# The output projection of layer 2: plain for 256 tokens, a block scheme of seven products for the rest

## The chip, the cores and the metric

The kernel runs on one core of one Trainium2 chip. Its engines work side by side and meet through semaphores: TensorE (PE, with its weight loads as PEld), VectorE (DVE), ScalarE (ACT), GpSimd (POOL) and SyncE (SP), whose queue issues most DMAs. Each engine does its instructions in the order in which they stand in its program. The metric is device time in microseconds of one launch; lower is better.

## The reference

One inference step of two layers for 1024 prompt tokens and 8 decode rows, all in float32. Layer 1 is a retention layer, layer 2 sliding-window attention with 16 heads of 64. What matters here is the end of layer 2:

```
def swa_layer(x, ...):
    ...
    o = swa_attend_prompt(q, k, v, sinks)       # (tokens, 1024)
    ...
    o = o * jax.nn.silu(gate)
    return x + o @ w_out, new_k, new_v          # w_out: 1024 x 1024
```

The projection has 1024 outputs, 1024 inputs and 1032 columns (1024 prompt tokens and 8 decode rows).

## The kernel before

Float32 products are made of three matmuls each: every operand is split into a high part (rounded) and a low part (the rest), and hi x hi, hi x lo and lo x hi are added up in PSUM (`proj`, L1710). ACT makes high parts, DVE or POOL the low parts. Data stand transposed, features on the partitions and tokens along the columns. `A_hi` and `A_lo` (SA in the profile) hold the eight k-tiles of 128 features of the moving operand.

Layer 2's attention is a loop written out by hand over 35 steps (L2504). In a step, scores of one block of 128 tokens are made (`att_s`), softmax runs on DVE, ACT and POOL (`att_e`, `att_p`, `att_r`), and for a block two steps back the values are multiplied (`att_o`) and gated (`att_out`, L2133) and split into hi and lo (`att_split`, L2143). Heads go in two groups: the outputs of group 0 (k-tiles 0 to 3) wait in DRAM as hi and lo (`oscr_h`, `oscr_l`) and are loaded back by `reload3` (L2253), since their place in `A_hi` still holds the layer's input; those of group 1 (k-tiles 4 to 7) are written to `A_hi` and `A_lo` directly. The decode rows' attention runs between the last steps (`STEPS`, L2495): `dec_scores`, `dec_soft`, `dec_pt`, `dec_o`, `dec_out` (L2247), which writes 8 columns of `A_hi`/`A_lo`.

Between the small matmuls of a step, `fill` gives PE pieces of larger work: first the input projections of layer 2, then the output projection, `so_all` (L2309). It has 24 tasks: 8 feature tiles of 128 x 3 token groups of 384, 384 and 264 columns, each 8 k-tiles x 3 matmuls. A task's accumulator is one PSUM bank (`pj`); `finish` (L2346) adds the residual (`xr`, L2359) and DVE transposes and SP or ACT stores the result (`so_y`, L2275) with four DMAs of 32 partitions. Six tasks run inside attention, eighteen behind it. Weights come in slots of 256 features (`wslot`, L1655): four loads of 256 KB, a high part by ACT (L1674), a low part by POOL (L1675), paced by `job` (L1683); three slots fit.

What is in no planner is set by the order in which this code calls the engines; the four engines besides PE also keep that order.

Of the kernel before, what the change touches and what calls it, by code (L numbers as in the profile page):

```python
# [15 lines left out]
NP = 1024  # L16
# [56 lines left out]
def _trunk(ctx, tc, nc, a):  # L73
# [23 lines left out]
    oscr_l = dp.tile([4, 128, NP], F32, name="oscr_l")  # L97
    pbs = dp.tile([8, 128, 640], F32, name="pbs")
# [1688 lines left out]
    atp = ctx.enter_context(tc.tile_pool(name="atp", bufs=1))  # L1787
# [345 lines left out]
    def att_out(u):  # L2133
        po, gt = u.po, G[u.g, u.ti]
        ot = atq[0].tile([128, 512], F32, name="ot", bufs=1)
        nc.vector.scalar_tensor_tensor(ot.rearrange("p (a y) -> p a y", a=4), po[:, :, 0:128], 0.5,
                                       gt[:, 512 * u.i:512 * u.i + 512].rearrange("p (a y) -> p a y", a=4),
                                       ALU.mult, ALU.mult)
# [108 lines left out]
    def dec_out():  # L2247
        nc.vector.scalar_tensor_tensor(god, god, 0.5, gdec2, ALU.mult, ALU.mult)
        nc.vector.tensor_copy(A_hi[:, :, NP:NT], god)
        nc.vector.tensor_tensor(A_lo[:, :, NP:NT], god, A_hif[:, :, NP:NT], ALU.subtract)  # L2250
        oready[2] = True

    def reload3(ti):  # L2253

        t0, t1 = TG[ti]
        t1 = min(t1, NP)
        for o_, src in ((A_hif, oscr_h), (A_lo.bitcast(F32), oscr_l)):
            nc.sync.dma_start(out=o_[:, 0:4, t0:t1], in_=src[:, :, t0:t1].rearrange("k p t -> p k t"))
# [6 lines left out]
    nso = [0]  # L2265
    attn = [True]
# [5 lines left out]
    pend_y, yds = [], []  # L2272
    LAST = ((7, 1), (7, 2))

    def so_y(ft, ti, yt):  # L2275
        t0, t1 = TG[ti]
        npr = min(t1, NP) - t0
        nch = npr // 128
        if (ft, ti) not in LAST:
            yo = atp.tile([128, 384], F32, tag="qs", name="yo", bufs=6)  # L2280
            nc.vector.transpose(yo[:, :npr], yt[:, :npr])
            st = nc.sync if attn[0] else nc.scalar
            for q in range(4):
                f0 = ft * 128 + 32 * q
                st.dma_start(
                    out=y_p[0, t0:t0 + npr, f0:f0 + 32].rearrange("(b r) c -> r b c", r=32),
                    in_=yo[32 * q:32 * q + 32, :npr].rearrange("r (b c) -> r b c", c=32))
            if ti == 2:
                nc.vector.transpose(yds[0][:, ft, :], yt[:, 256:288])
                if ft == 6:  # L2290
                    for q in range(4):
                        nc.scalar.dma_start(
                            out=y_s[:, 0, 0:896].rearrange("t (f c) -> t f c", c=128)[:, :, 32 * q:32 * q + 32],
                            in_=yds[0][32 * q:32 * q + 8])
            return
        pt = trp.tile([128, 512], F32, name="tr")
        for i in range(nch):
            tr(pt[:, i * 128:i * 128 + 128], yt[:, i * 128:i * 128 + 128], ident)
        if ti == 2:
            tr(pt[:8, 256:384], yt[:, 256:264], ident)  # L2300
# [320 lines left out]
```

## Time and profile before

| | us |
|---|---|
| median of 3 runs (1221.51 to 1223.53) | 1221.83 |
| the profiled execution | 1222.17 |
| its span, first to last instruction | 1220.3 |
| PE busy in the span | 1209.4 |
| 850 to 950: input projections of layer 2 begin, PE / DVE / ACT / POOL busy of 100 | 100.0 / 46.3 / 50.3 / 58.5 |
| 950 to 1146: attention, PE / DVE / ACT / POOL busy of 196 | 195.9 / 132.3 / 95.5 / 100.7 |
| 1146 to 1215: rest of the output projection, PE / DVE / ACT / POOL busy of 69 | 69.0 / 19.6 / 2.7 / 5.7 |

Times in rows are microseconds from the span's start. A group of instructions is told as line, engine, operation, what it writes and reads, count, then busy time and mean ns of one, then the engine's idle time just before them and what ended it. A busy PE is not PE at its peak: matmuls overlap, so starts are compared, not lengths. A wait for several things is put down to the one that came last.

### The profile page before, as it was taken

Reading aid. Unit: us, or ns where it says so; the run is one execution under the profiler, and the core shown is the slowest. Engines: PE = TensorE matmul, PEld = TensorE weight load, DVE = VectorE, ACT = ScalarE, POOL = GpSimd, SP = SyncE. Lnnn points to the kernel's source line nnn. Section 1 sums busy time; section 2 is a strip of 40 time slices with the busy share of each in tenths; the row PEclk is TensorE's granted clock in tenths of the full one; section 3 lists DMA queues with packets and bytes.
Section 4 is the critical chain, followed back from the end, with each engine's and each line's share of the span. In section 5 each row is a group of like instructions: output and inputs, shape, how many; then the busy total and the mean of one; then the engine's idle time right before and its main releaser. Section 6 shows DMA issues by size and latency. Waiting matters only on the chain.

```text
span 1220.3 us, 29346 instructions
## 1 busy us (share of the span) xinstructions
PE 1209.4 (99%) x11261; PEld 1148.0 (94%) x11261; DVE 733.2 (60%) x1425; ACT 590.2 (48%) x1518; POOL 693.1 (57%) x761
## 2 busy tenths in 40 slices
PE   8999999999999999999999999999999999999998
PEld 6999999999999999998888999999999999999998
DVE  6954656556656667357777455767435666677422
ACT  6533445535545556367877123446444545545100
POOL 5654544445527999968977145782656627654010
PEclk9999999999999999999999999999999999999999
DMA  6313866767676686365687894685531346246554
GB/s 227 110 52 118 247 190 214 223 205 220 205 237 185 194 242 188 109 199 185 216 251 215 246 261 151 195 250 155 137 117 65 115 133 174 90 140 181 135 125 86
DMA packets 260219, 213.18 MB, mean 175 GB/s; under 512 B 72953, under 2 KB 231093, under 8 KB 260062
## 3 DMA queue, kind: packets, MB, share of 16 engines
q1 hardware_dynamic: 215040, 180.72, 50.3%
q10 hardware_dynamic: 45038, 30.57, 8.3%
q8 instruction: 89, 1.46, 0.5%
q14 instruction: 52, 0.43, 0.1%
HBM read 139.10 MB, written 73.17 MB: 174 GB/s over the span
## 4 chain that ended last, share of the span: by engine, by line
PE 91%; DVE 3%; POOL 2%; DMA 1%; issue 1%; ACT 1%; ACTq 0%; SPq 0%; POOLq 0%; DVEq 0%
PE S L1346 10%; PE pj L1717 8%; PE b L340 8%; PE b L342 7%; PE b L341 7%; PE pj L1719 7%; PE pj L1718 7%; PE b L333 4%; PE b L334 4%; PE b L335 4%; PE xy L2070 2%; PE tr L109 2%; PE o L2128 2%; PE b L556 1%; PE S L341 1%; PE S L340 1%
## 5 line engine op out<-in xcount | busy, mean ns | idle before, releaser
L340 PE MATMUL b<-xh,woh 128*128 128x258 f32 x784 | 223.6, 285 | 0.0
L342 PE MATMUL b<-xh,wol 128*128 128x258 f32 x784 | 221.5, 283 | 0.1
L341 PE MATMUL b<-xl,woh 128*128 128x258 f32 x784 | 221.4, 282 | 0.0
L1717 PE MATMUL pj<-SA,wh 128*128 128x384 f32 (+1 forms) x576 | 189.6, 329 | 0.1
L1719 PE MATMUL pj<-SA,wl 128*128 128x384 f32 (+1 forms) x576 | 184.8, 321 | 0.0
L1718 PE MATMUL pj<-SA,wh 128*128 128x384 f32 (+1 forms) x576 | 184.2, 320 | 0.0
L340 PEld LDWEIGHTS b<-xh,woh 128*128 128x128 f32 x784 | 147.8, 188 | 4.1 <-issue 4.1
L341 PEld LDWEIGHTS b<-xl,woh 128*128 128x128 f32 x784 | 148.8, 190 | 0.0
L342 PEld LDWEIGHTS b<-xh,wol 128*128 128x128 f32 x784 | 148.2, 189 | 0.3 <-POOL wol L231 0.3
L231 POOL TENSOR_TENSOR wol<-raw,woh 128x512 fp32r<-128x512 f32 x51 | 66.4, 1310 | 119.8 <-ACT woh L226 117.4
L333 PE MATMUL b<-woh,xh 128*128 128x256 f32 x448 | 126.5, 282 | 0.0
L334 PE MATMUL b<-wol,xh 128*128 128x256 f32 x448 | 125.8, 281 | 0.0
L335 PE MATMUL b<-woh,xl 128*128 128x256 f32 x448 | 125.6, 280 | 0.0
L1717 PEld LDWEIGHTS pj<-SA,wh 128*128 128x128 f32 x576 | 108.5, 188 | 7.7 <-issue 5.8
L1718 PEld LDWEIGHTS pj<-SA,wh 128*128 128x128 f32 x576 | 109.0, 189 | 0.1
L1719 PEld LDWEIGHTS pj<-SA,wl 128*128 128x128 f32 x576 | 108.7, 189 | 0.0
L333 PEld LDWEIGHTS b<-woh,xh 128*128 128x128 f32 x448 | 84.3, 188 | 5.0 <-issue 2.9
L1675 POOL TENSOR_TENSOR wl<-wr,wh 128x512 fp32r<-128x512 f32 x48 | 63.1, 1322 | 40.9 <-ACT wh L1674 33.9
L335 PEld LDWEIGHTS b<-woh,xl 128*128 128x128 f32 x448 | 84.3, 188 | 0.0
L334 PEld LDWEIGHTS b<-wol,xh 128*128 128x128 f32 x448 | 84.3, 188 | 0.0
L226 ACT ACTIVATE woh<-s 128x512 fp32r<-128x512 f32 x88 | 54.1, 624 | 57.4 <-POOL s L216 23.4
L231 DVE TENSOR_TENSOR wol<-s,woh 128x512 fp32r<-128x512 f32 x88 | 68.0, 777 | 15.7 <-ACT woh L226 15.4
(516 smaller groups left out, 3133.6 us busy)
## 6 DMA issues: line engine op xcount, KB each, us to landing
raw<-in_w_in_ret_dram ACTq DMA_DIRECT2D x44, 512.0 KB
st<-in_state_ret_dram SPq DMA_DIRECT2D x64, 256.0 KB
out_dram<-st SPq DMA_DIRECT2D x64, 256.0 KB
vb<-vscr SPq DMA_DIRECT2D x64, 128.0 KB
evp<-qks SPq DMA_DIRECT2D x32, 256.0 KB
evx<-vsc SPq DMA_DIRECT2D x32, 256.0 KB
wr<-in_w_in_swa_dram SPq DMA_DIRECT2D x32, 256.0 KB
pbs<-pb SPq DMA_DIRECT2D x16, 320.0 KB
```

The costliest lines, as they stand in the source:

```text
L231: eng.tensor_tensor(lo, src_of(s, name, sub), hi.bitcast(F32), SUB)
L333: mm(dst, xh, wh, start=a and i == 0, stop=False, skip_group_check=True)
L334: mm(dst, xh, wl, start=False, stop=False, skip_group_check=True)
L335: mm(dst, xl, wh, start=False, stop=z, skip_group_check=True)
L340: mm(dst, wh, xh, start=a, stop=False, **sg)
L341: mm(dst, wh, xl, start=False, stop=False, **sg)
L342: mm(dst, wl, xh, start=False, stop=z, **sg)
L1346: mm(box[0], s.op[f"A{i + 1}{j + 1}", 0][w][:, k, :], xs_[t][x[j]][:, k, :], start=(xs_ is XH and w == 0 and j + k == 0), stop=(xs_ is XL ...
L1675: nc.gpsimd.tensor_tensor(box["lo"][:, js, :], raw, box["hi"].bitcast(F32)[:, js, :], ALU.subtract)
L1717: mm(ps, hi[:, k, fs], xh[:, k, t0:t1], start=first and k == ks[0], stop=False)
L1718: mm(ps, hi[:, k, fs], xl[:, k, t0:t1], start=False, stop=False)
L1719: mm(ps, lo[:, k, fs], xh[:, k, t0:t1], start=False, stop=last and k == ks[-1])
```

## The change

The 8 feature tiles for the first 256 tokens stay plain (`so_first`, 8 tasks of 256 columns, all inside attention). The other 776 columns (768 tokens and 8 decode rows) are cut into two halves H1 and H2 of 388. For each of four pairs of feature tiles ("sets", in the order 2, 3, 1, 0), weights are 2 x 2 blocks of 512 inputs x 128 outputs and the moving operand is 2 x 2 blocks of 512 inputs x 388 columns. A Strassen-Winograd scheme needs seven block products instead of eight (`so_prod`), each 4 k-tiles x 3 matmuls of 388 columns. In its products stand weight sums S1 to S4 and operand sums T1 to T4:

- `s_load` loads four blocks of raw weights, POOL adds them (`s_sum`), ACT makes the high part (`s_hi`), DVE the low one (`s_lo`).
- The operand sums are formed once, on DVE, from unsplit outputs (`x_sum`), and split by `t_hi` on ACT and `t_lo` on DVE. So that both groups' outputs can be had unsplit, `att_out` stores every block from token 256 on in a DRAM tensor `oraw`, and `reload3(2)` and `x_load` load it back. `att_out` writes those blocks by four multiplications instead of one.
- `so_ev` evicts a product into a partial sum or adds it to the residual; POOL adds two of the partial sums to residuals (`so_pre`). Results are transposed and stored on SP (`y_out`).
- Weights of the last two sets are loaded and split again (`again`), since the sums take one of the three slots.

The order of the products is `plan`; the first four need no sums and stand right behind the decode's last matmul. What else is to be done is put between products by the product's index (`todo`), and by the attention step (`SPREP`, `XPREP`).

```
-    nc.vector.scalar_tensor_tensor(ot.rearrange("p (a y) -> p a y", a=4), po[:, :, 0:128], 0.5, ...)
+        u.ot = ot.rearrange("p (l a x) -> p l a x", l=4, a=4)
+        for a_ in range(4):
+            nc.vector.scalar_tensor_tensor(u.ot[:, :, a_], po[:, a_, 0:128].rearrange("p (l x) -> p l x", l=4), 0.5,
+                                           gt[:, a_].rearrange("p (l x) -> p l x", l=4), ALU.mult, ALU.mult)
...
+            if u.c > 1:
+                nc.sync.dma_start(out=oraw[4 * u.g:4 * u.g + 4, :, ts_].rearrange("l p t -> p l t"),
+                                  in_=u.ot.rearrange("p l a x -> p l (a x)"))
...
+    def x_sum(x, dec=False):
+        cs, c2 = (slice(NM, NB), slice(NP, NT)) if dec else (slice(0, NM), slice(H2.start, NP))
+        if x == 1:
+            tt(TR_[1][:, :, cs], god[:, k0] if dec else A_lof[:, k0, c2], A_hif[:, k0, c2], SUB_)
+        elif x == 2:
+            tt(TR_[2][:, :, cs], god[:, k1] if dec else TR_[2][:, :, cs], TR_[1][:, :, cs], SUB_)
...
+    JJ = (("A11", None, 0, True), ("S2", 2, 1, True), ("S1", 1, 2, True), ("A12", None, 0, False),
+          ("S3", 3, 1, True), ("S4", None, 2, True), ("A22", 4, 1, False))
...
+        for k in range(4):
+            mm(ps, hi[:, k], xh[:, k], start=first and k == 0, stop=False, skip_group_check=True)
+            mm(ps, hi[:, k], xl[:, k], start=False, stop=False, skip_group_check=True)
+            mm(ps, lo[:, k], xh[:, k], start=False, stop=k == 3, skip_group_check=True)
...
+    plan = [(0, 0), (1, 0), (0, 3), (1, 3), (0, 1), (0, 2), (0, 4), (0, 5), (0, 6)] + [
+        (1, j) for j in (1, 2, 4, 5, 6)] + [(n, j) for n in (2, 3) for j in range(7)]
...
+    XPREP = {(33, 1): ((x_sum, 1),), (34, 0): ((x_load, 2),), (34, 1): ((x_sum, 3), (x_sum, 2))}
...
+    for n, i0 in ((1, 4), (2, idx[1, 2]), (3, idx[2, 2])):
+        for k, fn, *args in ((0, s_load, n), (1, y_load, n), (2, s_sum, n, "S1"), (2, s_sum, n, "S3"), (3, s_sum, n, "S2"),
...
```

How instructions move is seen at three places. First DVE at the end of attention, from the decode's softmax to its last step, before (`sq<-pj,xr` is the eviction of a task, `pm` the decode's probabilities):

```order
L2212 TENSOR_TENSOR rbc<-rbc,ddec 128x16
L2159 TENSOR_TENSOR SA<-ot,SA 128x4x128
L2359 TENSOR_TENSOR sq<-pj,xr_15631 128x384
L2281 STREAM_TRANSPOSE yo<-sq 128x384
L2227 COPY pm_15849<-xy 8x128
L2359 TENSOR_TENSOR sq<-pj,xr_15733 128x384
L2281 STREAM_TRANSPOSE yo<-sq 128x384
L2248 SCALAR_TENSOR_TENSOR gdec<-gdec 128x64
```

and now (`kk<-SA` is the operand sum x_sum(1), the three with `V_11398` are x_sum(3) and x_sum(2), which read the reload x_load(2)):

```order
L2368 TENSOR_TENSOR kk<-SA 128x4x380
L2171 TENSOR_TENSOR SA<-ot,SA 128x4x128
L2317 TENSOR_TENSOR sq<-pj,xr_15800 128x256
L2297 STREAM_TRANSPOSE sq<-sq 128x256
L2239 COPY pm_15988<-xy 8x128
L2317 TENSOR_TENSOR sq<-pj,xr_15857 128x256
L2297 STREAM_TRANSPOSE sq<-sq 128x256
L2417 TENSOR_TENSOR wl<-rq,wh 128x4x128
L2374 TENSOR_TENSOR acc<-V_11398,SA 128x2x380
L2374 TENSOR_TENSOR rbc<-V_11398,SA 128x2x380
L2370 TENSOR_TENSOR V_11398<-V_11398,kk 128x4x380
L2317 TENSOR_TENSOR sq<-pj,xr_15955 128x256
```

One sum stands ahead of the first of these evictions, and a low part and three sums ahead of the last.

Second, SP's queue at the same place, before:

```order
L2342 DMA xr_15822<-xscr 128x384
L2285 DMA out_dram<-yo 32x12x32 x4
L2342 DMA xr_15865<-xscr 128x384
L2285 DMA out_dram<-yo 32x12x32 x4
L2342 DMA xr_15917<-xscr 128x384
L2285 DMA out_dram<-yo 32x12x32 x4
```

and now (`rq` are raw weights for the sums, `V_11398<-oraw` is x_load(2), `t4h<-oraw` x_load(4)):

```order
L2162 DMA oraw<-ot 128x4x128
L2404 DMA rq<-in_w_out_swa_dram 128x4x128 x2
L2404 DMA rq_15938<-in_w_out_swa_dram 128x4x128
L2309 DMA xr_15955<-xscr 128x256
L2292 DMA out_dram<-sq 32x8x32 x8
L2362 DMA V_11398<-oraw 128x4x380
L2404 DMA rq<-in_w_out_swa_dram 128x4x128
L2292 DMA out_dram<-sq 32x8x32 x4
L2362 DMA t4h<-oraw 128x4x388
```

The reload x_load(2) stands behind the stores of two tasks, x_load(4) behind those of a third.

Third, the products of sets 1 and 2. On POOL stood low parts of weights (`wl<-wr,wh`) and small fills:

```order
L2356 MEMSET sq 128x24 x2
L1675 TENSOR_TENSOR wl<-wr,wh 128x512 x3
L2356 MEMSET sq 128x24
L1675 TENSOR_TENSOR wl<-wr,wh 128x512
L2356 MEMSET sq 128x24 x4
```

and now POOL has, for set 2 (`rq` are S1, S3 and S2, the rows of 388 the pre-additions of set 1):

```order
L1676 TENSOR_TENSOR wl<-wr,wh 128x512 x3
L2534 TENSOR_TENSOR rbc<-rbc,V_11398 128x388
L1676 TENSOR_TENSOR wl<-wr,wh 128x512
L2536 TENSOR_TENSOR rbc<-rbc,xp 128x388
L2537 TENSOR_TENSOR acc<-acc,xp 128x388
L2410 TENSOR_TENSOR rq_16120<-rq_16120,rq_16122 128x512
L2410 TENSOR_TENSOR rq_16122<-rq_16121,rq_16122 128x512
L2410 TENSOR_TENSOR rq_16121<-rq_16120,rq_16121 128x512
```

while SP's queue there reads (the first row is the last raw block of set 1, `wr` are the weights loaded again for set 2, the next three rows its raw blocks):

```order
L2404 DMA rq_16120<-in_w_out_swa_dram 128x4x128
L2292 DMA out_dram<-sq 32x12x32 x16
L1669 DMA wr<-in_w_out_swa_dram 128x2x256 x3
L2404 DMA rq_16120<-in_w_out_swa_dram 128x4x128
L2404 DMA rq_16122<-in_w_out_swa_dram 128x4x128
L2404 DMA rq_16121<-in_w_out_swa_dram 128x4x128
L1669 DMA wr<-in_w_out_swa_dram 128x2x256
```

The loads that set 2 needs stand behind sixteen stores, and its sums on POOL behind four low parts and three pre-additions.

More of the change, by code (lines that the diff above doesn't have):

```diff
@@ new lines, in _trunk, with y_store, y_out @@
+    NPL = 256
+    NB = (NT - NPL) // 2
+    H1, H2 = slice(NPL, NPL + NB), slice(NPL + NB, NT)
+    def y_store(eng, ft, t0, yo, n):
+        for q in range(4):
+            f0 = ft * 128 + 32 * q
+            eng.dma_start(out=y_p[0, t0:t0 + n, f0:f0 + 32].rearrange("(b r) c -> r b c", r=32),
+                          in_=yo[32 * q:32 * q + 32, :n].rearrange("r (b c) -> r b c", c=32))
+    def y_out(eng, ft, t0, src, n):
+        yo = io("sq", 4)
+        nc.vector.transpose(yo[:, :n], src)
+        y_store(eng, ft, t0, yo, n)
@@ new lines, in so_first, with x_ahead, finish @@
+    def so_first():
+        early, xrs, todo = [], [], list(range(8))
+        def x_ahead():
+            if len(xrs) < 2 and todo:
+                ft = todo.pop(0)
+                xr = iop2.tile([128, 384], F32, tag="xr", bufs=2, name="xr2")
+                xrs.append(xr)
+                xp_ = slice(64 * (ft % 2), 64 * (ft % 2) + 64)
+                nc.sync.dma_start(out=xr[:, :NPL], in_=xscr[ft // 2, xp_, :, 0:NPL].rearrange("p u t -> (p u) t"))
+        def finish():
+            ft, ps = early.pop(0)
+            for ks in ([4, 5], [6, 7]):
+                proj(ps[:, :NPL], so_slots[ft // 2], ft % 2, 0, NPL, first=False, last=ks[-1] == 7, ks=ks)
+                yield 6 * NPL / 2400.0
+            yt = io("sq", 4)
+            nc.vector.tensor_tensor(yt[:, :NPL], ps[:, :NPL], xrs.pop(0)[:, :NPL], ALU.add)
+            nso[0] += 1
+            x_ahead()
+            if ft == 1:
@@ L2375, in so_all @@
                     yield 1e9
                 yield from finish()
-            while ti == 2 and not oready[2]:
-                yield 1e9
-            yield from start(ft, ti)
+            so_ahead(ft // 2 + 1)
+            x_ahead()
+            x_ahead()
+            ps = pjp.tile([128, 512], F32, tag="pj", name="pj")
+            job()
+            for k in range(4):
+                proj(ps[:, :NPL], so_slots[ft // 2], ft % 2, 0, NPL, first=(k == 0), last=False, ks=[k])
+                yield 3 * NPL / 2400.0
@@ new lines, in t_lo, with y_load, blk @@
+    def t_lo(x):
+        for h, l_, r in t_parts(x):
+            tt(l_, r, f32(h), SUB_)
+    def y_load(n):
+        for i in range(2):
+            ft = 2 * SETS[n] + i
+            y = Y[n % 2][i]
+            xp_ = slice(64 * (ft % 2), 64 * (ft % 2) + 64)
+            nc.sync.dma_start(out=y[:, 0:768], in_=xscr[ft // 2, xp_, :, NPL:NP].rearrange("p u t -> (p u) t"))
+            nc.sync.dma_start(out=y[:, 768:776], in_=xdec[ft // 2, xp_].rearrange("p u t -> (p u) t"))
+    def blk(n, i, par):
+        return Y[n % 2][i][:, NB * par:NB * par + NB]
```

372 lines of the change are left out of this document (249 added, 123 removed).

## The prediction

> **What bounds the kernel now.** I read the page first, then the waits of PE over layer 2, then the table by windows, then the timeline around the end of attention. The first lines are the page's span and busy times, the only row of PE's waits from 860 us to the end, and three windows of the output projection after attention (columns: window, length, then busy us and count of PE, weight loads, DVE, ACT, POOL, then granted clock, DMA share, GB/s).
>
> ```profile
> span 1220.3 us, 29346 instructions
> PE 1209.4 (99%) x11261; PEld 1148.0 (94%) x11261; DVE 733.2 (60%) x1425; ACT 590.2 (48%) x1518; POOL 693.1 (57%) x761
> PE tr L109 <- DVE sq L2359: 0.2, 1, 0.2
> 1140.00:1160.00 20.00, 20.00 (x113) 19.59 (x112) 5.85 (x13) 1.04 (x5) 0.24 (x2) 0.91 0.39 82
> 1160.00:1180.00 20.00, 20.00 (x131) 20.00 (x130) 5.35 (x12) 0.46 (x1) 0.00 (x0) 1.00 0.54 128
> 1180.00:1200.00 20.00, 20.00 (x146) 20.00 (x145) 6.40 (x16) 1.95 (x4) 5.46 (x9) 1.00 0.48 103
> ```
>
> PE waits for nothing in layer 2 except 0.2 us at the end. The stretch from 1140 to the end is PE alone: in 20 us DVE has 5 to 6 us of work, ACT 2 at most, POOL nearly none in two windows of three. So whatever takes columns away from PE here shortens the kernel at the full rate, and whatever makes PE wait lengthens it at the full rate. The next rows are starts on PE's timeline (start, length, engine, line), with DVE's last eviction.
>
> ```profile
> 1139.89 0.60 PE L109 MATMUL xy<-ident,rbc 128*128 128x128 f32 x4
> 1143.44 1.96 PE L2240 MATMUL xy<-pm,vc 128*128 128x16 f32 x16
> 1145.25 0.42 PE L1717 MATMUL pj<-SA,wh 128*128 128x384 f32 x1
> 1146.39 0.52 PE L1717 MATMUL pj<-SA,wh 128*128 128x384 f32 x1
> 1149.58 0.44 PE L1718 MATMUL pj<-SA,wh 128*128 128x384 f32 x1
> ...
> 1150.03 0.34 PE L1717 MATMUL pj<-SA,wh 128*128 128x384 f32 x1
> 1166.32 0.28 PE L1717 MATMUL pj<-SA,wh 128*128 128x264 f32 x1
> 1172.17 0.34 PE L1717 MATMUL pj<-SA,wh 128*128 128x384 f32 x1
> 1215.14 0.43 DVE L2359 TENSOR_TENSOR sq<-pj,xr 128x264 f32<-128x264 f32 x1 [2.37 <-PE pj L1719]
> ```
>
> **The columns that go.** From 1150.03 to 1166.32 there are 93 matmuls of 384 columns, 0.175 us each; from there to 1172.17 there are 48 of 264, 0.122 us each. That is 0.000444 us per column, so 388 columns cost 0.177 us and 256 cost 0.118 us. After the decode's last matmul (L2240) PE's program now has 255 matmuls of 384 and 192 of 264: 44.7 + 23.4 = 68.1 us. With the 10 slow ones from 1146.39 to 1149.58 (0.32 us apart instead of 0.175, 1.45 us in all) that fills 1145.25 to 1215.0, as the last eviction at 1215.14 confirms. The change leaves 28 products of 12 matmuls of 388 columns there: 336 x 0.177 = 59.4 us. Inside attention, between the same neighbours, 129 matmuls of 384 (22.6 us) become 192 of 256 (22.7 us), nothing. So 8.7 us of PE go, and without any wait the profiled 1222.2 us (span 1220.3 and 1.9 around it, 0.3 above the median of 1221.83) would become 1213.5. The end after the last matmul stays about as long: eviction, transposes, copy, store.
>
> **What the change adds.** These rows price it (line, engine, operation, count, then busy us and mean ns): vector work by width, then sums on POOL, conversions on ACT, then issues on SP with the conversion that waited for one.
>
> ```profile
> L231 DVE TENSOR_TENSOR wol<-s,woh 128x512 fp32r<-128x512 f32 x88 | 68.0, 777 | 15.7 <-ACT woh L226 15.4
> L2136 DVE SCALAR_TENSOR_TENSOR ot<-o,gt 128x512 f32<-128x512 f32 x16 | 10.9, 683 | 13.3 <-PE o L2128 13.3
> L2359 DVE TENSOR_TENSOR sq<-pj,xr 128x384 f32<-128x384 f32 x16 | 8.9, 556 | 35.1 <-PE pj L1719 34.0 <-DMA xr<-xscr 1.1
> L2359 DVE TENSOR_TENSOR sq<-pj,xr 128x264 f32<-128x264 f32 x8 | 3.5, 433 | 13.4 <-PE pj L1719 11.7 <-DMA out_dram<-yo 1.8
> L2281 DVE STREAM_TRANSPOSE yo<-sq 128x384 f32<-128x384 f32 x15 | 8.7, 579 | 0.5
> L207 POOL TENSOR_TENSOR s<-raw 128x512 f32<-128x512 f32 x22 | 32.3, 1469 | 1.7 <-DMA raw<-in_w_in_ret_dram 1.3
> L840 POOL TENSOR_TENSOR ql<-evp,qh 128x256 fp32r<-128x256 f32 x28 | 20.5, 733 | 0.0
> L1675 POOL TENSOR_TENSOR wl<-wr,wh 128x512 fp32r<-128x512 f32 x48 | 63.1, 1322 | 40.9 <-ACT wh L1674 33.9 <-DVE sq L1955 6.1 <-POOL ndp L2057 0.5
> L226 ACT ACTIVATE woh<-s 128x512 fp32r<-128x512 f32 x88 | 54.1, 624 | 57.4 <-POOL s L216 23.4 <-POOL s L210 11.0 <-PE b L334 7.4
> L439 ACT ACTIVATE junk<-xq 128x1024 f32<-128x1024 f32 x4 | 4.2, 1055 | 1.9 <-DMA xq<-in_x_prompt_dram 1.9
> 1132.23 0.57 DVE L2200 SCALAR_TENSOR_TENSOR rbc<-o,r,ddec 128x129 f32<-128x129 f32 x2
> 1121.91 1.62 SPq L1668 DMA_DIRECT2D wr<-in_w_out_swa_dram  x2
> 1125.11 0.63 ACT L1674 ACTIVATE wh<-wr 128x512 fp32r<-128x512 f32 x1 [1.06 <-DMA wr<-in_w_out_swa_dram]
> 1127.08 0.43 SPq L2258 DMA_DIRECT2D SA<-oscr_h  x1
> 1140.41 1.86 SPq L2285 DMA_DIRECT2D out_dram<-yo  x4
> ```
>
> A DVE sum costs about 0.16 us and 1.03 ns per element (433 ns at 264, 556 at 384): 1.7 us for 1,520 elements, 2.3 at most by three times 777 ns. ACT takes 1.6 us for 1,552 (1,055 ns for 1,024). POOL takes 1.47 us for a 512-wide sum, 1.3 for a low part, about 1.1 for 388 (between 733 at 256 and 1,469 at 512). A 256 KB load is used 3.2 us after its issue (1121.91 to 1125.11). Four stores hold SP's queue for 1.86 us.
>
> All these engines have room; what counts is where the work stands in queues that keep their order. I follow PE's five meetings with them.
>
> (1) End of attention.
>
> ```profile
> 1128.41 1.26 POOL L2102 TENSOR_TENSOR s<-s,sm 128x640 f32<-128x640 f32 x1
> 1138.52 0.18 DVE L2212 TENSOR_TENSOR rbc<-rbc,ddec 128x16 f32<-128x16 f32 x1
> 1139.21 0.55 DVE L2359 TENSOR_TENSOR sq<-pj,xr 128x384 f32<-128x384 f32 x1
> ```
>
> The eviction at 1139.21, which frees a bank, gets the first operand sum (1.7 us) ahead of it, and the strided gating costs 4 x 0.285 instead of 0.683 (0.5 us more). It ends near 1142; PE would want the bank after the four transposes of 1139.89, at 1140.2. One more conversion also stands on POOL ahead of the last normalisation (L2102), 1.3 us, and three more ahead of the decode's power. 2 to 5 us of PE wait; I take 3.
>
> (2) The second product, (1,0), needs the bank of the last plain task, and that eviction now stands on DVE behind the sums x_sum(3) and x_sum(2), which need the reload of the raw outputs. The reload stands on SP behind eight stores. From the eviction before: transposes, copy, eviction, transposes on DVE overlap the first four stores; both sets of stores are issued after 0.45 + 2 x 1.86 = 4.2 us, the reload's issue 0.43, its landing 3.2 for 256 KB and about 2 more for 778 KB, the sums 0.95 + 0.95 + 1.7, the eviction 0.43: 13.9 us. PE fills 24 x 0.118 + 2.2 (decode) + 2.1 (one product) = 7.1 of it. It waits 6.8; 4.8 if the reload lands like 256 KB, 8 with the sums at 777 ns per 512. I take 6.
>
> (3) From that eviction DVE has, in order, a transpose, the decode's three small ones, three low parts of weight sums (2.3 us), four tiny sums: 4.3 us; ACT's first high part is out at 5.5, DVE's low parts at 7.2, 9.0, 10.9, the fourth sum at 12.7. PE does three products (6.4 us), then goes on at 7.2: a wait of 1 at most. But the next weights' loads stand on SP behind the stores of the eviction that follows the fourth sum: 13.8 on DVE, 15.7 on SP, landed at 19.5. POOL sums S1, S3, then two pre-additions, then S2: 25.9; high and low part: 27.3. PE, after six products, is there at 18.2. It waits 9, with (3)'s first part 10; 7.4 with 2.3 us landings and POOL at 1.3, 11 with the prices at their highest.
>
> (4) Set 2 needs S2 again, and POOL reaches it after four conversions of weights loaded again, three pre-additions and two sums. From one S2 to the next: on SP one load, sixteen stores (7.4 us), then the first weight piece, landed at 11.4; ACT 0.6; POOL three conversions 16.0, a pre-addition 17.1, a fourth conversion, whose load waits for the first one's buffer, 18.4, two pre-additions 20.6, three sums 25.0. PE's seven products are 14.9. It waits 10; at least 2.7, since POOL's own 4 x 1.47 + 4 x 1.32 + 3 x 1.1 = 14.5 and one reload of 3.2 are 17.7.
>
> (5) Set 3 the same with eight stores instead of sixteen ahead: 22.8 against 14.9, 8 us; at least 2.7. At the dearer prices of POOL and DVE (4) and (5) cost about 1 us more each.
>
> [...] From the row alone I take 2 us (0 to 5.8, four times 1.45), since the next meeting depends mostly on SP and POOL.
>
> Sum: 1222.2 - 8.7 + 3 + 6 + 10 + 10 + 8 + 2 = 1252.5. With the low ends (2, 4.8, 7.4, 2.7, 2.7, 0) it is 1233; with the high ends (5, 8, 11, 11, 9, 5.8) 1263.
>
> **The rivals.** First, *the cover holds*: the four products that need no sums, 8.5 us, hide the operand sums, and the loads land ahead; PE never waits long and the time is 1213.5. For it: 5 to 6 us of DVE in 20, idle POOL, DMA at half. Against it: the orders on DVE and SP in (2) and (3). It decides if the reload is issued before about 1141, when DVE is not held. Chance 0.13.
>
> Second, *only the hand-over costs*: (1) to (3) at their low ends, then each set's weights are ready in time, because stores do not hold SP: 1222.2 - 8.7 + 14.2 = 1227.7, between 1222 and 1233. Chance 0.14, of which 0.03 within 0.2% of before.
>
> Third, *DVE becomes the bound*. Here is what the same low part costs when POOL works on its neighbour.
>
> ```profile
> L1219 DVE TENSOR_TENSOR w<-rb,w 128x512 fp32r<-128x512 f32 x8 | 10.6, 1327 | 1.8 <-ACT w L1214 1.8
> ```
>
> After the reload DVE has about 51 us of work at the prices above. If its sums with two inputs in SBUF cost 1,327 ns per 512 instead of 777, some 14 us of low parts and sums grow by 10, and those on the chains (1 to 2 us in each of five) go to PE: 1252.5 + 10 = 1262 and more. Chance 0.07 above 1264. [...]
>
> **How the numbers follow.** My forecast (all five waits) has 0.66, between 1233 and 1264; its value is 1252. The range 1222 to 1264 leaves out the first rival (0.13) and the third (0.07). Faster by over 0.2% (what a measurement of this kernel can tell) 0.13, within 0.03, slower 0.84.
>
> **What would show it.** In the profile after: matmuls of 388 columns 0.177 us apart; PE idle before L2466 of the second product, released by DVE sq; before the first product of set 1 with S2, and of sets 2 and 3, released by DVE or ACT, 8 to 10 us each; the page's PE share at 96 to 97%. I am wrong if PE has no wait above 3 us after 1140, if the waits are there but before other products, or if products are slower than 2.1 us with no wait.

## The result and the profile after

The changed kernel took 1272.42 us (median of 5 runs, 1268.28 to 1272.99), the kernel before 1222.08 (5 runs, 1221.51 to 1223.53). The ratio is 1.0399, 95% interval 1.0379 to 1.0419: slower by 50 us. The forecast was 1252, between 1222 and 1264. The sign is right, the size is not, and the time lies outside the range.

These are the page's first lines, then PE's waits from 860 us to the end (engine, line, what it waited for: us in all, times, longest), then three rows of the table by windows.

```profile
span 1270.4 us, 29489 instructions
PE 1214.1 (96%) x11211; PEld 1149.0 (90%) x11211; DVE 767.6 (60%) x1502; ACT 609.4 (48%) x1547; POOL 739.4 (58%) x794
```
```profile
PE sb L2466 <- DVE rbc L2485: 11.8, 1, 11.8
PE pj L1718 <- DVE sq L2317: 10.7, 3, 6.5
PE sb L2466 <- DVE yt L2485: 6.6, 2, 4.9
PE pj L2466 <- DVE sq L2317: 6.5, 1, 6.5
PE sb L2466 <- ACT kk L2476: 3.3, 1, 3.3
PE pj L2466 <- ACT V L2476: 1.3, 1, 1.3
...
```
```profile
1130.00:1140.00 10.00, 6.96 (x151) 6.12 (x149) 1.78 (x7) 3.10 (x8) 2.45 (x2) 1.00 0.92 303
1160.00:1180.00 20.00, 12.23 (x51) 11.39 (x51) 13.25 (x20) 7.80 (x13) 2.29 (x5) 0.66 0.47 142
1200.00:1220.00 20.00, 8.24 (x44) 7.92 (x43) 3.91 (x7) 3.15 (x5) 9.10 (x9) 0.73 0.60 158
```

Where PE had one wait of 0.2 us, it now has 41 us of them, at the end of attention (L1718) and before the products (L2466). And in the two later windows the granted clock is 0.66 and 0.73 instead of 1.00: PE pays for a wait a second time, in the matmuls behind it.

Two marks divide the loss: the start of the last score matmuls (L2070 before, L2072 after) and the decode's last matmuls (L2240, L2252).

```profile
1119.85 0.78 PE L2070 MATMUL xy<-kk,qs 64*32 64x160 f32 x32
```
```profile
1121.66 0.78 PE L2072 MATMUL xy<-kk,qs 64*32 64x160 f32 x32
1158.39 0.28 PE L2252 MATMUL xy<-pm,vc 128*128 128x16 f32 x1
```

Up to the first mark the changed kernel is 1.8 us later. Little of its code there is new (some tasks of 256 columns, the stores of raw outputs, the gating in four parts), and the first mark lies between 1119.2 and 1122.7 in the experiments too, which is more than those 1.8 us, so they are taken for scatter. From mark to mark it takes 36.7 us instead of 23.6 (to 1143.44): **13.1 us lost at the end of attention**. From the second mark to the end it takes 112.0 instead of 76.9: **35.1 us lost in the products**, where the columns alone should have gained 8.7. Together 50.0, against 50.1 between the spans. In the runs that left a stretch as it was, the first came out at 35.4 to 38.2 and the second at 110.2 to 112.0; smaller differences than that mean nothing in a single run.

**End of attention.** The longest wait there, followed back over the queues (start, length, engine, line, what, then idle time before it and what ended it):

```profile
1127.91 1.21 SPq L2273 DMA_DIRECT2D SA<-oraw  x2
1130.01 2.32 SPq L1669 DMA_DIRECT2D wr<-in_w_out_swa_dram  x3
...
1138.12 1.29 ACT L1675 ACTIVATE wh<-wr 128x512 fp32r<-128x512 f32 x2 [6.71 <-DMA wr<-in_w_out_swa_dram]
1138.83 1.27 POOL L1676 TENSOR_TENSOR wl<-wr,wh 128x512 fp32r<-128x512 f32 x1 [6.89 <-ACT wh L1675]
1140.05 1.26 POOL L2104 TENSOR_TENSOR s<-s,sm 128x640 f32<-128x640 f32 x1
1141.34 0.84 DVE L2112 STREAM_TRANSPOSE R<-s 128x640 f32<-128x640 f32 x1 [8.09 <-POOL s L2104]
1143.00 0.41 DVE L2317 TENSOR_TENSOR sq<-pj,xr 128x256 f32<-128x256 f32 x1
1143.47 0.58 PE L1718 MATMUL pj<-SA,wh 128*128 128x256 f32 x1 [6.51 <-DVE sq L2317]
```

Read it upwards. PE waits for a bank; its eviction stands on DVE behind a softmax transpose, that waits for POOL's normalisation (L2104), which stands on POOL behind a weight conversion, that waits for ACT's half of it, which waits 6.7 us for a weight load. Until that load is there, from 1137.0 to 1138.1, none of these engines works; four queues hold one late load between them. In the other runs that left this stretch as it was, the same wait took 3.4 to 6.5 us.

**The products.** The wait of 11.8 us, before the last product of set 1, followed back in the same way:

```profile
1196.23 8.30 SPq L2292 DMA_DIRECT2D out_dram<-sq  x16
1204.58 1.50 SPq L1669 DMA_DIRECT2D wr<-in_w_out_swa_dram  x3
1209.60 0.37 SPq L1669 DMA_DIRECT2D wr<-in_w_out_swa_dram  x1
...
1215.08 0.63 ACT L1675 ACTIVATE wh<-wr 128x512 fp32r<-128x512 f32 x1 [4.94 <-DMA wr<-in_w_out_swa_dram]
1215.79 1.26 POOL L1676 TENSOR_TENSOR wl<-wr,wh 128x512 fp32r<-128x512 f32 x1 [2.81 <-ACT wh L1675]
1217.01 1.00 POOL L2536 TENSOR_TENSOR rbc<-rbc,xp 128x388 f32<-128x388 f32 x1
1218.04 0.56 DVE L2485 TENSOR_TENSOR rbc<-sb,rbc 128x388 f32<-128x388 f32 x1 [14.78 <-POOL rbc L2536]
1218.66 0.69 PE L2466 MATMUL sb<-t4h,wh 128*128 128x388 f32 x1 [11.76 <-DVE rbc L2485]
1219.14 0.53 PE L2467 MATMUL sb<-t4l,wh 128*128 128x388 f32 x1
1219.47 0.53 PE L2468 MATMUL sb<-t4h,wl 128*128 128x388 f32 x1
```

Sixteen stores, then the reloaded weights (L1669, those of the *next* set), their fourth piece only when a buffer is free, the conversion, and behind it on POOL the pre-addition (L2536) that set 1's own eviction needs. The last two rows show the second price: 0.33 us from matmul to matmul, where 0.177 is the rate.

Set 0's last product has a wait of 4.9 us of the same kind, behind set 1's weight sums on POOL. The 3.3 us in set 2 are an eviction on ACT behind set 3's reloaded weights:

```profile
1231.65 0.63 ACT L1675 ACTIVATE wh<-wr 128x512 fp32r<-128x512 f32 x1 [7.19 <-DMA wr<-in_w_out_swa_dram]
1232.18 0.48 ACT L2476 ACTIVATE kk<-sb 128x388 f32<-128x388 f32 x1
```

The 6.5 us before the second product are the ones that step (2) described:

```profile
1155.40 4.75 SPq L2292 DMA_DIRECT2D out_dram<-sq  x8
1160.25 0.40 SPq L2362 DMA_DIRECT2D V<-oraw  x1
...
1165.13 0.95 DVE L2374 TENSOR_TENSOR acc<-V,SA 128x760 f32<-128x760 f32 x1 [6.68 <-DMA V<-oraw]
1169.58 0.41 DVE L2317 TENSOR_TENSOR sq<-pj,xr 128x256 f32<-128x256 f32 x1
1170.05 0.69 PE L2466 MATMUL pj<-SA,wh 128*128 128x388 f32 x1 [6.49 <-DVE sq L2317]
```

And the end after the last matmul grew. In this timeline 24 stores are spread over 19.6 us of SP's queue, and DVE's last copies are 3.5 us behind PE's transposes. The last row, of experiment 1, names what such a copy waits for: the buffer that it writes is still being stored.

```profile
1262.31 0.63 PE L110 MATMUL pj<-ident,rbc 128*128 128x128 f32 x4 [0.56 <-issue]
1266.01 0.29 DVE L2517 COPY sq<-pj 128x128 f32<-128x128 f32 x1 [3.60 <-issue]
...
1223.44 0.29 DVE L2512 COPY sq<-pj 128x128 f32<-128x128 f32 x1 [3.39 <-DMA out_dram<-sq]
```

From the last product to the end it is 8.6 us now (1262.31 less 0.56 of idle time, to 1270.4), 5.3 before (1215.0 to 1220.3).

### The profile page after: what moved, and what is told of

The parts are those of the page before. It is cut to its first block, busy times and chain, and to the rows that moved or that the text cites. A ratio compares the mean times of both kernels' runs of the same rounds, so it can differ in the third digit from the quotient of the medians.

```text
span 1270.4 us, 29489 instructions
## 1 busy us (share of the span) xinstructions
PE 1214.1 (96%) x11211; PEld 1149.0 (90%) x11211; DVE 767.6 (60%) x1502; ACT 609.4 (48%) x1547; POOL 739.4 (58%) x794
## 4 chain that ended last, share of the span: by engine, by line
PE 73%; POOL 8%; DMA 7%; DVE 6%; issue 3%; SPq 2%; ACT 1%; ACTq 0%; POOLq 0%; DVEq 0%
PE S L1347 9%; PE b L341 5%; PE b L343 5%; PE b L342 5%; PE pj L1718 5%; PE pj L1720 4%; PE pj L1719 4%; PE b L334 4%; PE b L335 4%; PE b L336 4%; DMA wr<-in_w_out_swa_dram 2%; PE tr L110 2%; PE xy L2072 2%; PE S L341 1%; PE S L342 1%
## 5 line engine op out<-in xcount | busy, mean ns | idle before, releaser
L1718 PE MATMUL pj<-SA,wh 128*128 128x384 f32 (+2 forms) x448 | 146.3, 327 | 10.8 <-DVE sq L2317 10.7
L1720 PE MATMUL pj<-SA,wl 128*128 128x384 f32 (+2 forms) x448 | 141.5, 316 | 0.0
L1719 PE MATMUL pj<-SA,wh 128*128 128x384 f32 (+2 forms) x448 | 141.0, 315 | 0.0
L1718 PEld LDWEIGHTS pj<-SA,wh 128*128 128x128 f32 x448 | 84.9, 190 | 19.0 <-DVE sq L2317 11.3
L1676 POOL TENSOR_TENSOR wl<-wr,wh 128x512 fp32r<-128x512 f32 x56 | 74.1, 1334 | 45.9 <-ACT wh L1675 38.9
L1719 PEld LDWEIGHTS pj<-SA,wh 128*128 128x128 f32 x448 | 85.2, 190 | 0.0
L1720 PEld LDWEIGHTS pj<-SA,wl 128*128 128x128 f32 x448 | 85.0, 190 | 0.0
```

Of the source, the lines that this page charges most:

```text
L1676: nc.gpsimd.tensor_tensor(box["lo"][:, js, :], raw, box["hi"].bitcast(F32)[:, js, :], ALU.subtract)
L1718: mm(ps, hi[:, k, fs], xh[:, k, t0:t1], start=first and k == ks[0], stop=False)
L1719: mm(ps, hi[:, k, fs], xl[:, k, t0:t1], start=False, stop=False)
L1720: mm(ps, lo[:, k, fs], xh[:, k, t0:t1], start=False, stop=last and k == ks[-1])
```

## The experiments

All are single runs unless a number is given; the kernel before ran at 1219.7 to 1223.0 beside them. "The attention stretch" is the time between the two marks, "the tail" that from the second mark to the end: 36.7 and 112.0 us in the changed kernel, 23.6 and 76.9 in the one before.

**1. What the products cost without sums.** Every product reads plain weights and plain operands.

```diff
-        if name in WOP:
-            i, jj = WOP[name]
-            hi, lo = [v[:, 4 * jj:4 * jj + 4, 128 * i:128 * i + 128] for v in so_slots[SETS[n]][0:2]]
...
+        if True:
+            i, jj = WOP.get(name, (1, 1))
+            hi, lo = [v[:, 4 * jj:4 * jj + 4, 128 * i:128 * i + 128] for v in so_slots[SETS[n % 2]][0:2]]
+        xh, xl = [v[:, slice(0, 4), H1] for v in (A_hi, A_lo)]
...
-        for fn, *args in SPREP.get((m, s), ()) + XPREP.get((m, s), ()):
-            fn(*args)
...
-            todo.setdefault(i + 2, []).append((so_pre, (n, j)))
...
-    for n in (2, 3):
+    for n in ():
```

> Left out: all weight sums, all operand sums, the pre-additions and the second load of weights; every product reads plain weights and plain operands of its set's size, so the 28 products, their evictions, stores and the attention part stay. Theory W (the products are slow only because PE waits, and because the clock is low after each wait): no wait above 1 us after the decode's last matmul, products 2.13 us each from the second on, and that part lasts 59.4 + about 7 instead of 110 us; the time is 1228 (1270 - 30 of waits - 12 of slow matmuls). Rival R (the products are slow by themselves, by what DVE, POOL and the DMAs do beside them): spacing stays above 0.19 us in places without a wait before them, 1235 or more. The 13 us that the end of attention lost are still there in both; if they vanish, the sums at the end of attention caused them, and the time is 1215.

1229.86 us. After the second mark PE has no wait but the 0.5 us before the last transposes, and from the eighteenth matmul on they are 0.177 us apart:

```profile
...
PE pj L110 <- DVE rbc L2502: 0.5, 1, 0.5
```

The tail is 71.5 us, 5.4 less than before: the 8.7 of the columns are there, less the later end. Theory W holds, R falls. Of the first seventeen matmuls ten are 0.32 us apart with no wait in front of them, like the ten in the kernel before: they stand behind the decode's small matmuls. The attention stretch is still 34.1.

**2. Clock.** Matmuls that nobody reads fill two of the waits.

```diff
+        if (n, j) in ((0, 6), (1, 6)):
+            banks[n + 1, 1] = bp.tile([128, 512], F32, tag="b1", bufs=2, name="sb")
+            for _ in range((22, 56)[n]):
+                mm(banks[n + 1, 1][:, 0:NB], so_slots[SETS[n]][0][:, 0, 0:128], A_hi[:, 0, H1], start=True, stop=True, skip_group_check=True)
```

> Added: 22 and 56 matmuls of 388 columns whose results nobody reads, ahead of the last products of sets 0 and 1, so that PE works through most of its 4.9 and 11.8 us there. Theory K (a wait of over 3 us leaves the clock at half for the next 8 to 15 matmuls, whatever the next work is): the matmuls after those two waits are 0.18 us apart instead of 0.32, and the time falls by 3 to 4 us, to 1268.5. Rival (the slow matmuls have to do with what the product reads, or with DVE and POOL beside them): they stay 0.32 apart and the time is the same within 1 us, 1271.5 to 1273.

1267.95 us, the tail 109.4. This timeline shows the 22 (L2455) and the product behind them:

```profile
1188.05 4.06 PE L2455 MATMUL sb<-SA,wh 128*128 128x388 f32 x22
1191.95 0.34 PE L2470 MATMUL sb<-t4h,wh 128*128 128x388 f32 x1
1192.13 0.34 PE L2471 MATMUL sb<-t4l,wh 128*128 128x388 f32 x1
```

0.18 us apart, where the changed kernel has 15 intervals of 0.32 behind this wait and 12 behind the next. Theory K holds at these two places: being idle is what slows the matmuls, not what they read nor what runs beside them. Those 27 intervals cost 4.3 us; the tail got 2.6 shorter, since part of the time that PE won it then waited for POOL and ACT. How large that part is a single run does not tell (unchanged tails differ by 1.8 us), and the time as a whole is only 0.3 us below the shortest of the changed kernel's runs.

**3. The second load of weights.** Left out, with its conversions.

```diff
-            hi, lo = [v[:, 4 * jj:4 * jj + 4, 128 * i:128 * i + 128] for v in so_slots[SETS[n]][0:2]]
+            hi, lo = [v[:, 4 * jj:4 * jj + 4, 128 * i:128 * i + 128] for v in so_slots[SETS[n % 2]][0:2]]
...
-    for n in (2, 3):
+    for n in ():
         i0 = idx[n - 2, 6] + 1
```

> Left out: the second load and conversion of the weights for the last two sets (their plain products read the first two sets' weights); their weight sums stay. Theory P' (set 1's pre-additions stand on POOL behind conversions that wait for these loads): the 11.8 us wait falls to 4 or less, sets 2 and 3 wait like set 0, about 5 each at most, and the time is 1254 to 1260. Theory L (what holds all of it are the stores on SP, whoever stands behind them): the weight sums' loads are still behind 16 stores, the wait falls to 7 to 9 only, 1263 to 1268.

1253.37 us, the tail 92.8: 19.2 less, more than P' gave it. PE's waits after the second mark:

```profile
PE sb L2466 <- DVE yt L2485: 5.3, 1, 5.3
PE pj L2466 <- DVE sq L2317: 5.2, 1, 5.2
PE sb L2466 <- ACT wh L2413: 2.6, 1, 2.6
```

The 11.8 and the 3.3 are gone, of sets 2 and 3 only 2.6 and 0.3 are left. The stores and the weight sums are all still there, so stores on SP alone (theory L) do not make these waits.

**4. Its order, nothing left out.** Three pieces are loaded ahead of the 16 stores (`ahead`), the slot is taken when it is free (`again`), and the pieces are converted behind the pre-additions (`piece`, whose first conversion is followed by the fourth load).

```diff
-        i0 = idx[n - 2, 6] + 1
-        todo.setdefault(i0, []).insert(0, (again, (SETS[n],)))
-        for i in range(i0, i0 + 5):
-            todo.setdefault(i, []).extend([(job, (1,))] * 2)
+        i0, c0, fp = (idx[0, 6] + 1, 15)[n - 2], idx[n - 1, 2] + 2, SETS[n]
+        todo.setdefault(i0, []).insert(0, (again, (fp,)))
+        todo.setdefault((5, 15)[n - 2], []).insert(0, (ahead, (fp,)))
+        for i, k in enumerate((0, 0, 1, 2)):
+            todo.setdefault(c0 + k, []).append((piece, (fp, i)))
```

> Nothing is left out. The reloaded weights of set 2 are loaded four products earlier, ahead of 16 stores on SP's queue, and those of both sets are converted behind their neighbour's pre-additions and first sums on POOL instead of ahead of them. Theory P' (the second load costs 19 us because POOL's queue holds pre-additions and weight sums behind conversions whose loads are late): the waits of 11.8 and 3.3 us shrink to 5 in all, the waits stay as without that load elsewhere, and the time is 1256 to 1261. Theory Q (POOL's own work, four conversions of 1.3 us more per set, is what is missing from the set's 15 us, whatever the order): they move to the plain products of sets 2 and 3 and the time is 1266 or more.

1258.19 us, the tail 99.7: 12.3 of the 19.2 come back by order alone (on SP's queue and on POOL together), and most of what is left shows as a wait of a plain product for its own weights. Here are two rows of POOL and that wait:

```profile
1206.50 1.28 POOL L2410 TENSOR_TENSOR rq<-rq,rq 128x512 f32<-128x512 f32 x1 [3.31 <-DMA rq<-in_w_out_swa_dram]
1209.56 2.94 POOL L1676 TENSOR_TENSOR wl<-wr,wh 128x512 fp32r<-128x512 f32 x2
1211.32 0.69 PE L2468 MATMUL sb<-SA,wl 128*128 128x388 f32 x1 [4.11 <-POOL wl L1676]
```

The time is in the range of P'. That the rest is Q, the conversions' own work, is not shown: the low parts stand on POOL behind a weight sum (L2410), before which POOL is idle for 3.3 us, waiting for a raw block whose load stands on SP behind the sixteen stores. It is the same kind of wait again, one place further.

**5. Pre-additions on DVE.**

```diff
-            nc.gpsimd.tensor_tensor(blk(n, 1, 0), blk(n, 1, 0), pp_, ALU.add)
+            tt(blk(n, 1, 0), blk(n, 1, 0), pp_, ALU.add)
```

(and the two others)

> Only the three pre-additions of each set go from POOL to DVE. Theory P (a set's last product waits because the pre-additions stand on POOL behind weight work that waits for loads): the waits of 4.9 and 11.8 us before the last products of sets 0 and 1 go, and nothing of their size comes: 1252 to 1256 with the clock. Theory L (the loads are late, behind stores on SP's queue, and whoever needs them waits): the waits move to the first product of the next set that uses a weight sum, and the time falls by 6 us at most, 1264 to 1270.

1263.74 us, the tail 105.4, 6.6 less. The waits before the last products of sets 0 and 1 go; a wait of 3.3 comes before set 1's first product with a weight sum, and this one before set 2's:

```profile
1216.56 0.69 PE L2466 MATMUL sb<-t2h,wh 128*128 128x388 f32 x1 [8.32 <-ACT wh L2413]
```

As theory L had it, though the time is just below its range: the wait moves by two products to the next user of the late work. The pre-additions were only the first in POOL's queue to need it.

**6. Stores on ACT's queue.**

```diff
-            y_out(nc.sync, f0, NPL, Y[n % 2][0][:, 0:384], 384)
+            y_out(nc.scalar, f0, NPL, Y[n % 2][0][:, 0:384], 384)
```

(and the three others of `so_ev`)

> Only the output stores of the four sets go from SP's queue to ACT's. Theory L (weight loads stand behind stores on SP): in set 1 the reloaded weights are issued about 8 us earlier, the 11.8 us wait falls to about 3, the 4.9 us one to about 3, the 24 stores at the end leave SP alone, and the time is 1254 to 1260. Theory P (POOL's order decides): the waits stay within 2 us, 1268 to 1272. If ACT's own conversions now wait behind stores, the time rises above 1272.

1273.29 us, the tail 115.6, longer by 3.6. The wait of 4.9 fell to 2.0 and that of 11.8 to 7.6, as L had it, but 6.5 and 5.5 us came before the first products of sets 1 and 2 with a weight sum: ACT's conversions now stood behind the stores. Both theories missed that sum, though the last sentence of the expectation named its cause.

**7. The operand sums' load on ACT's queue,** ahead of its place behind eight stores on SP's.

```diff
-    XPREP = {(33, 1): ((x_sum, 1),), (34, 0): ((x_load, 2),), ...
+    XPREP = {(33, 1): ((x_sum, 1),), (33, 2): ((x_load, 2),), ...
-        nc.sync.dma_start(out=d, ...
+        (nc.scalar if x == 2 else nc.sync).dma_start(out=d, ...
```

> Only the raw outputs' load for the operand sums goes from SP's queue, where it stands behind eight stores, to ACT's queue ahead of the fold into products. By the prediction's step (2) (the last plain task's eviction stands on DVE behind two operand sums, which wait for that load, which waits for the stores): it is issued near 1151 to 1155 instead of 1160.3, the 6.5 us wait before the second product falls to 0 to 2, with 2 us of slow matmuls, and the time is 1264 to 1267. Rival: the load is late by its bytes or by the write of the raw outputs before it; the wait stays above 4 and the time above 1269.

1262.29 us, the tail 105.1, 6.9 less. It is issued at 1150.8, lands at 1157.6, and the second product hardly waits:

```profile
1161.59 0.45 PE L2466 MATMUL pj<-SA,wh 128*128 128x388 f32 x1 [0.45 <-DVE sq L2317]
```

Step (2) of the prediction is shown by this: the chain of stores, load, sums, eviction, bank. The product behind now waits 3.9 instead of 1.3.

**8. The end of attention: the fourth pair's weights.** Not loaded, not converted.

```diff
         for fp in range(len(so_slots), n):
+            if fp == 3:
+                so_slots[3] = so_slots[2]
+                continue
```

> Left out: the load and the conversion of the fourth pair of weights (its tasks and products read the third pair's). Theory A (four more weight pieces in the last 20 us of attention, which wait for their loads on ACT and POOL ahead of the last softmax steps, are the 13 us by which the decode's last matmul is later): it ends at about 1150 instead of 1160 and the time is 1260. Theory B (the order on DVE, with the first operand sum and the gating by parts, is it): it stays within 3 us of 1160, the time within 3 us of 1270. Theory C (the reload of 1.5 MB of raw outputs delays what is loaded beside it, the softmax's own transfers too): 1263 to 1268.

1263.13 us, the attention stretch 29.4, 7.3 less, the wait of 6.5 us gone; waits of 2.2 and 1.7 are left. Theory A for more than half of the 13.1, B and C not for that part.

**9. The reload of raw outputs behind the weight pieces.**

```diff
-        while pend_r:
+        while pend_r and pend_r[0] < 2:
+    STEPS ... (32, 0): (lambda: reload3(pend_r.pop(0)),)
-    XPREP = {(33, 1): ((x_sum, 1),), (34, 0): ((x_load, 2),), ...
+    XPREP = {(34, 0): ((x_load, 2), (x_sum, 1)), ...
```

> The reload of 1.5 MB of raw outputs comes on SP's queue behind the fourth pair's weight pieces instead of ahead of them, and the first operand sum moves behind it. Theory C (the pieces land 6 us late because the reload is in front of them, and the last normalisation waits on POOL behind the conversions): the pieces land about 4 us after their issue, the waits of 6.5 and 2.4 us at the end of attention shrink by 3 to 5 us together, the time is 1266 to 1269. Theory A (the pieces themselves are late, because their buffers and slot come free late): within 2 us of 1272. If the reload now holds up the decode's load or the operand sums, the 6.5 us wait before the second product grows and the time is above 1273.

1267.57 us, the attention stretch 33.5, 3.2 less. The first two pieces, issued at 1128.69 and 1129.21, are now used from 1133.19 and 1133.83 on, 4.5 and 4.6 us later; in the changed kernel it was 8 us. So the reload in front of them is what made them late, as C had it, and the wait of 6.5 is 1.9. In the whole stretch that is only 1.9 below the shortest unchanged one, and in the time 0.7 below the shortest run; experiments 10 and 11 tell more.

**10 and 11. What is left of the attention stretch,** on the bare kernel of experiment 1: without the fourth pair (the edit of 8), and then without the last reload too.

> Left out: all sums as in the bare kernel, and the fourth pair's load and conversion. The stretch from the last score matmuls to the decode's last (23.6 us before, 36.7 with the change, 34.1 in the bare kernel, 29.4 without the fourth pair alone) tells what is left of the 13 us. Theory A+ (fourth pair 7, sums 2 to 3, reload of raw outputs 3, as separate links): 26 to 28 us, and the time is 1221 to 1223. Theory A only (the fourth pair is all but scatter): 24 to 25 us, 1219. If the gating by parts or the order on DVE is a link, it stays at 29 or more and the time at 1225.

1223.32 us; the stretch is 27.6.

```diff
-            reload3(pend_r.pop(0))
+            ti = pend_r.pop(0)
+            if ti < 2:
+                reload3(ti)
```

> As the bare kernel without the fourth pair, and the reload of 1.5 MB of raw outputs left out too. Theory A+: the stretch falls by 2 to 4 us more, to 23.5 to 25, about that of the kernel before, and the time is 1218 to 1220. Theory A only: no change from the kernel without the reload's removal, within 1.5 us. Either way it shows the bound of this scheme if every sum, load and conversion were hidden: 1222.2 - 8.7 + 3 for the later end = 1216.5 at best.

1219.34 us; the stretch is 27.7. (The two times differ by 4.0: 2.8 lie ahead of the first mark, 1.2 in the tail, where the first of them has ten slow matmuls behind the decode's and the second has none.) So the fourth pair costs 6.5 to 7.3 of the 13.1 (34.1 to 27.6, 36.7 to 29.4). The sums in attention come out at 1.8 to 2.6 (29.4 to 27.6, 36.7 to 34.1), which is within the scatter; the traces name their share all the same: a wait of 1.7 to 1.8 us for the eviction behind the first operand sum stands in each of the eight runs that have this sum right ahead of it, and in none of the three without sums. (Experiment 9 moves the sum away; there the same eviction waits 1.8 us for its residual's load.) The reload costs nothing once the fourth pair is away: by itself it is no link, it makes that pair's loads later.

4 us are still there with all three gone. In both traces they are a wait of 2.1 us and slow matmuls behind it, 0.21 us apart instead of 0.12. These rows are of the second:

```profile
1123.24 0.63 ACT L1675 ACTIVATE wh<-wr 128x512 fp32r<-128x512 f32 x1 [1.49 <-DMA wr<-in_w_out_swa_dram]
1123.78 0.19 ACT L2080 ACTIVATE s<-snk 128x4 f32<-128x4 f32 x1
1124.01 0.82 DVE L2093 TENSOR_REDUCE mx<-s 128x4 f32<-128x644 f32 x1 [1.73 <-ACT s L2080]
1126.07 0.41 DVE L2322 TENSOR_TENSOR sq<-pj,xr 128x256 f32<-128x256 f32 x1
1126.54 0.39 PE L1718 MATMUL pj<-SA,wh 128*128 128x256 f32 x1 [2.14 <-DVE sq L2322]
```

It is the same kind of chain: an eviction stands on DVE behind a softmax step, which waits for a small instruction on ACT, which stands behind the conversion of an earlier weight piece whose load is late. The changed kernel has it too, as its wait of 2.4 us at 1128.59. In the kernel before, that ACT instruction (L2078) runs at 1118.96, ahead of the two conversions that wait for loads there. Which edit put it behind them was not tested.

The last of these kernels does no sum, no second load and no fourth pair, and is 2.0 us faster than the kernel before beside it (1221.32). These are single runs, and those of the kernel before differ by as much. Its tail is 6.9 us shorter (70.0 for 76.9), and its attention stretch takes 4.1 of that back. With all those loads and sums hidden, this scheme has about 3 us to give here; nearly 7 only if that wait went as well.

**12. All repairs that leave nothing out:** those of 4, 7 and 9, and one of the last set's stores on ACT's queue.

> All repairs that leave nothing out, together: the reload of raw outputs behind the weight pieces (3 us alone), the operand sums' load on ACT's queue (7 us alone), the reloaded weights early and behind the pre-additions (12 to 16 if theory P' holds), and one of the last set's stores on ACT's queue (0 to 2). If the causes are separate links of one chain in time, their gains add: 1246 to 1251. If each only uncovers the next one, it is 1255 or more. In neither case is it below 1222, since the fourth pair's conversions at the end of attention (7), set 0's and set 1's late weight sums and the slow matmuls after the waits that are left stay.

1254.71 us (4 runs, 1252.8 to 1258.48), ratio 1.0282, interval 1.0261 to 1.0303. The tail is 97.0, the attention stretch 34.4. The sum of the single gains (3 + 7 + 12 to 16) was not reached: 17.7 us came of 22 to 26. Its trace has the 4.8 us before set 0's last product that no repair touched, 6.0 for the plain products' reloaded weights, a new wait of 2.6 at the decode's first matmul, and 2.4 that are left before the second product. No kernel that computes everything came below 1222, and none of the runs points to one: with the sums and the second load all gone, experiment 1 was still at 1229.86.

## Why the prediction came out too low

- **The columns** (-8.7): right. Products without waits run at 0.177 us per matmul, as reckoned from 0.000444 us per column.
- **The end** ("stays about as long"): wrong by 3.3 us. The last set's stores stand in one queue, and the last copies wait for a buffer that is being stored.
- **(1), the end of attention** (3 taken, 5 at most): 13.1. This is the step that failed most. It said "One more conversion also stands on POOL ahead of the last normalisation (L2102), 1.3 us": the place is right, the price is that of the instruction alone. In the trace after, that conversion follows 6.9 us of idle POOL, because its load was late; experiment 8 takes 7.3 us away with it. Here an instruction in an in-order queue cost what it waited for, 6.9 us, and not what it ran, 1.27. In the trace, 10.7 of the 13.1 are three waits: 6.5 by this conversion, 1.7 behind the first operand sum, as the prediction priced that sum, and 2.4 by an earlier conversion on ACT with a late load, in front of a softmax step; slow matmuls after them are another 2.
- **(2), the second product** (6): 6.5, by the chain described; experiment 7 removes it. One price in the chain was too low: the sum x_sum(2) took 2.68 us instead of 1.7, with POOL at work beside it from 1166.00 to 1168.07; in experiment 7 it took 1.74. The 2 us for the bytes above 256 KB are an estimate for which the prediction has no row; its 5.2 us from the load's issue to the first sum were 4.9 in the trace after (1160.25 to 1165.13) and 6.8 in experiment 7 (1150.77 to 1157.61).
- **(3), (4), (5), the sets** (10, 10, 8): 6.2, 11.8 and 6.0, so 24.0 for 28 in all (the 3.3 us in set 2 counted to set 3, whose reload makes them; experiment 3 takes them away). That PE would wait at each change of sets, because work for the next set stands behind stores, was right; who waits was not, and "the waits are there but before other products" was one of the prediction's own signs of being wrong. It had PE wait for S2. In fact the last product of the old set waits first, as its bank's eviction needs a pre-addition that stands on POOL behind the next set's work. S2 is the next in line, as experiment 5 shows. With the wait at another place, it is partly luck that 24.0 comes near 28. For the 2.3 us landings at the low end of (3) the prediction has no row either; in the trace after, a raw block that POOL waited for was used 3.2 us after its issue (1195.75 to 1198.92).
- **The clock** (2 taken, 5.8 at most): 8.4. The changed kernel has 67 intervals of 0.25 to 0.6 us among the products, 9.9 us above 0.177 each, where the row of before had 1.45. Four waits of 3.3 to 11.8 us are followed by 11 to 15 slow intervals each, 1.6 to 2.3 us every time; the granted clock behind the longest of them was 0.50 from 1218.66 to 1222.40 and 1.00 from 1222.70 to 1226. The 2 us of the sum were the author's estimate from the ten slow matmuls of before, which stand behind small matmuls and no wait (granted clock 0.50 from 1146.39 to 1149.58). That a wait slows the matmuls behind it was not shown by the kernel before, where PE's only wait in layer 2 was one of 0.2 us, and no run shows 2 us for all the waits together. The prediction put the term low "since the next meeting depends mostly on SP and POOL"; its upper end, 1.45 for each of four waits, was nearer. Experiment 2 shows that the idle time does it: with PE at work through two of the waits, the matmuls behind them were 0.18 us apart.

The account: 1252.5 by the prediction, +10.1 for (1), +0.5 - 4.0 for the other waits, +6.4 for the clock, +3.3 for the end, and 1.8 of scatter ahead of the first mark, is 1270.6; 1272.4 was measured. Most of the rest, 1.3, is in the waits themselves: idle time counts from the end of a matmul, but without a wait the next one starts before that end (0.34 us long and 0.18 apart in the rows of experiment 2), and from start to start seven waits among the products are 0.15 to 0.35 us longer than their idle time and 0.177.

Of the rivals, "the cover holds" and "only the hand-over costs" fall with the 11.8 us that set 2's weights cause. "DVE becomes the bound" falls too, though the time is on its side of 1264: DVE is busy for 4 to 13 us in each 20, and the long waits go back to loads and to POOL. Its price is real, though. Of the sixteen low parts of weight sums after 1155 us, the five that took 1.0 to 1.25 us all ran while POOL worked; the ten that ran mostly without POOL took 0.65 to 0.7, as did one beside it. With x_sum(2) that is some 3 us of DVE time, 0.9 of it on the way to a wait of PE.

## What to carry to other kernels

When PE is 99% busy, a scheme that saves matmuls is priced by what it makes PE wait for: here 8.7 us of saved columns met 41 us of waits and 8 of slow clock. Price a new instruction in an in-order queue with the latest input it can have, and follow who stands behind it on that queue, through every queue, to PE; one late load passed through ACT, POOL, DVE and a bank. And ask of each resource that an algorithm needs (here weight slots for four pairs and their sums) whether it fits at once: loading the weights of the last two sets again was the dearest single part, 19 us.

## What was not expected of the hardware

- Matmuls are slow behind some waits of 2 us (0.21 us apart instead of 0.12 at 256 columns, 0.32 instead of 0.18 at 388), and the length of a wait alone does not tell which. Every wait of 2.9 us or more from 1100 us on, in all these traces, was followed by slow matmuls, at once or within thirteen; this is the shortest of them (experiment 7), with 18 intervals of 0.32 us behind it:

```profile
1185.66 0.66 PE L2466 MATMUL sb<-t4h,wh 128*128 128x388 f32 x1 [2.92 <-DVE yt L2485]
```

  Behind waits of up to 1.75 us the spacing stayed at 0.18 (0.12 at 256 columns). In between both happen: 1.80 and 2.02 us were followed by slow matmuls (at 1153.83 in experiment 3, at 1255.14 in experiment 6), 2.41, 2.64 and 2.82 were not (at 1128.59 in the changed kernel, 1213.65 in experiment 3, 1144.10 in experiment 1). And behind the decode's small matmuls slow ones stand without any wait. What decides is open.

- Weight pieces of 256 KB, used 3.2 us after their issue in the trace of before, took 7.6 to 8.1 us behind 1.5 MB of other loads (issued at 1130.01, 1130.82 and 1131.96, used from 1138.12, 1138.78 and 1139.57 on), at 303 GB/s and a DMA share of 0.92 from 1130 to 1140. With the 1.5 MB behind them they took 3.8 to 4.6 (experiment 9).
- Moving transfers from one issuing queue to another was no free repair: with the stores of the sets on ACT's queue, waits of 6.5 and 5.5 us for ACT's conversions came before products, and the tail grew by 3.6 us (experiment 6), while a single early load there took 6.9 us off it (experiment 7).
